# The order of part products in the last down unit of each MLP round

## The chip, the cores and the metric

The kernel runs on one core of a Trainium2 chip. The metric is device time in microseconds (us), as the median of several executions. TensorE does the matrix products (PE in the profile, its weight loads PEld), VectorE (DVE), ScalarE (ACT) and GpSimd (POOL) do the rest, and SyncE (SP) issues most transfers.

## What is computed

One inference step of a decoder with two layers, for 512 prompt tokens and 64 sample tokens that share all weights (576 columns, model width 1024). Each layer is a mixer and an MLP, each with a norm ahead and a residual behind:

```
hp = hp + yp                       # mixer 0: retention and gating, mixer 1: windowed attention
hp = hp + sqrelu_mlp(rmsnorm(hp, norm_mlp[l]), mlp_w_up[l], mlp_w_down[l])

def sqrelu_mlp(h, w_up, w_down):
    return jnp.square(jax.nn.relu(h @ w_up)) @ w_down     # width 1024 -> 4096 -> 1024
```

The change is in the product with `w_down`.

## The kernel before

Activations lie with features on the 128 partitions and the 576 tokens along the free axis, in two halves of 288 (`TH`). Every matrix product is made in float32r from two parts per operand: a value is `hi` (rounded by a cast on ScalarE) plus `lo` (the rest, a subtraction on VectorE), and hi·hi, hi·lo and lo·hi are added up in PSUM. `block` (L304) does this for a whole 576-column product, `product` (L311) for one of 288 columns.

Weights arrive as raw tiles (three buffers). Each piece of 128x512 is a job: ScalarE casts it to `whi` (L248), VectorE subtracts to get `wlo` (L259). `whi` and `wlo` have six buffers each (`NW_ = 6`), so the cast of job n+6 waits until TensorE has read job n to the end. `ahead_to(used + 5)` after each product prepares one job more; sums of weight blocks (L233, on VectorE) stand ahead of some casts.

Each MLP runs in four rounds of 1024 hidden features. A round has eight up products of 48 matmuls and then four down units `m = 0..3`. A down unit is a block product in the Strassen manner: seven products P1, P5, P6, P2, P7, P3, P4, each of 12 matmuls of 128x128 on 128x288: four blocks `k` of hidden features times three pairs of parts. `w` is the job's `whi` and `wlo`, `x(k)` the parts `ahi` and `alo` of block k's squared activations. Between products ScalarE copies accumulators (L548, L554, L561) and VectorE adds them into the residual `h` (L512). The first unit (`m = 0`) takes blocks 0 to 2 first and block 3 later. The last round of the second MLP has no down units, so there are seven rounds with a last unit (`m = 3`): four in the first MLP, three in the second. Rounds are counted here from 0 within the first MLP.

In the last round of the first MLP the norm of mixer 1 is prepared between the products: for each chunk c of `h`, ScalarE makes `xhi` (L391) and the square (L401), VectorE makes `xlo` (L392), and GpSimd adds the square into `ssq` (L407). Then mixer 1 starts with a `block` product over the eight chunks and with `norm.finish()`, which casts `ssq` to `sqh` (ScalarE, L212), subtracts `sql` (VectorE, L213) and multiplies both by a matrix of ones (L370, L371). `bq` (L958) is a small scaling of a bias on VectorE that belongs to mixer 1.

Inside the MLPs VectorE and ScalarE run in the order in which the code is written; TensorE, and everything in mixer 1, runs in the order of a scheduler.

Of the kernel before, what the change touches and what calls it, by code (L numbers as in the profile page):

```python
# [18 lines left out]
P = 128  # L19
D = 1024  # L20
KC = D // P
# [99 lines left out]
def hybrid_step(ctx: ExitStack, tc: tile.TileContext, a, o):  # L121
    nc = tc.nc
# [11 lines left out]
    def acc_tile():  # L134
        return ps.tile([P, 2, 512], F32, name="acc", tag="acc", bufs=2)

    def m_tile(name="m"):
        return ps.tile([P, 512], F32, name=name, tag="m", bufs=4)
# [12 lines left out]
    for c in range(KC):  # L151
        t = keep.tile([P, T], F32, name=f"h{c}")
# [119 lines left out]
    def ahead_to(n):  # L272

        n = min(n, len(jobs))
        while len(parts) < n or owed:
            while summed[0] < min(len(parts) + 2, len(jobs)):
                job, i = jobs[summed[0]]
                k = SUMS.get(job)
                if k:
                    total(k, i)  # L280
                summed[0] += 1
            if len(parts) < n:
                prepare()
            split_low()
        load_to(done[0] + 3)

    def take(n):
        i = used[0]
        used[0] += n
        split_to(i + n)  # L290
        return parts[i:i + n]
# [12 lines left out]
                nc.tensor.matmul(out, lhsT=w_, rhs=x_[:, hf if isinstance(hf, slice) else half(hf)],  # L304
                                 start=(start and si == 0), stop=(stop and si == 2))

    def product(out, w, x, ks_, start, stop):

        for si, (wi, xi) in enumerate(((0, 0), (0, 1), (1, 0))):
            for k in ks_:  # L310
                nc.tensor.matmul(out, lhsT=w[wi][:, k * P:(k + 1) * P], rhs=x(k)[xi],  # L311
                                 start=(start and k == ks_[0] and si == 0),
                                 stop=(stop and k == ks_[-1] and si == 2), skip_group_check=True)

    def cut(piece, k):
        return [w[:, (k % 4) * P:(k % 4 + 1) * P] for w in piece[k // 4]]
# [176 lines left out]
    def down_unit(acts, m, first, between, nxt):  # L493


        operand = {"P1": 0, "P2": 2, "P3": 1, "P5": 3, "P6": 4, "P7": 5, "P4": 6}
        row1, row2 = h[2 * m], h[2 * m + 1]
        both = acc_tile()
        x, v = both[:, 0, 0:TH], both[:, 1, 0:TH]
        n2, n1 = slice(0, TH), slice(TH, T)  # L500

        def bank(name):
            return m_tile(name)[:, 0:TH]

        def run(n, out, start, stop=True, ks_=range(4), w=None, ahead=NW_ - 1):
            w = w or take(1)[0]
            product(out, w, lambda k: [t[:, operand[n]] for t in acts[k]], ks_, start, stop)
            if ahead:
                ahead_to(used[0] + ahead)

        def to_h(row, cols_, src, op):
            nc.vector.tensor_tensor(out=row[:, cols_], in0=row[:, cols_], in1=src, op=op)  # L512

        def shared(src):
            to_h(row1, n2, src, ALU.add)
            to_h(row2, n2, src, ALU.subtract)

        if first:

            y, g, f = bank("y"), bank("g"), bank("f")  # L520
            early = [("P1", x), ("P2", y), ("P3", g), ("P5", f)]
            ws = take(4)
            for (n, out), w in zip(early, ws):
                run(n, out, True, False, range(3), w, 0)
            for (n, out), w in zip(early, ws):
                run(n, out, False, True, [3], w, 0)
                if n == "P1":
                    nc.scalar.copy(out=v, in_=x)
            to_h(row1, n1, y, ALU.add)
            to_h(row1, n2, g, ALU.add)  # L530
            ahead_to(used[0] + 2)
            run("P6", x, False, ahead=0)
            shared(f)
            z = bank("z")
            nc.scalar.copy(out=z, in_=x)
            ahead_to(used[0] + 2)
            to_h(row1, n1, v, ALU.add)
            to_h(row1, n2, x, ALU.add)
            w_ = bank("w")
            run("P4", w_, True, ahead=3)  # L540
            to_h(row2, n1, w_, ALU.subtract)
            run("P7", z, False, ahead=4)
            to_h(row2, n1, z, ALU.subtract)
            to_h(row2, n2, z, ALU.subtract)
            return
        run("P1", x, True)
        y = bank("y")
        nc.scalar.copy(out=y, in_=x)  # L548
        f = bank("f")
        run("P5", f, True)  # L550
        shared(f)
        run("P6", x, False)
        z = bank("z")
        nc.scalar.copy(out=z, in_=x)  # L554
        for c in between[0:1]:
            nxt.chunk(c)
        run("P2", y, False)
        to_h(row1, n1, y, ALU.add)
        run("P7", z, False)
        w_ = bank("w")  # L560
        nc.scalar.copy(out=w_, in_=z)  # L561
        to_h(row2, n2, z, ALU.subtract)
        for c in between[1:2]:
            nxt.chunk(c)
        run("P3", x, False)
        to_h(row1, n2, x, ALU.add)
        run("P4", w_, False)
        to_h(row2, n1, w_, ALU.subtract)
# [774 lines left out]
```

## Time and profile before

| | |
|---|---|
| median of 3 runs | 1242.55 us (1240.84 to 1244.82) |
| the profiled execution | 1244.38 us, span 1242.3 us |
| TensorE busy (matmul / weight load) | 97% / 96% |
| VectorE, ScalarE, GpSimd busy | 69%, 47%, 15% |
| mean granted TensorE clock | 0.993 of full speed |
| chain that ended last | TensorE 82%, VectorE 10%, ScalarE 3%, issue 3%, DMA 2% |
| matmuls in `product` (L311) | 2352, of which 588 in last units |

The timeline lists instructions by their start; the length of a matmul there includes its way through the array, so the pace is read from the distance of two starts. A number in brackets at the end of a row is idle time of that engine just before it, with what ended it.

### The profile page before, as it was taken

To read this page: it belongs to the slowest core of one execution; us is meant where nothing else is said; L and a number is where in the kernel's file an instruction comes from. 1 tells how busy PE (TensorE), PEld (TensorE's weight loads), DVE (VectorE), ACT (ScalarE), POOL (GpSimd) and SP (SyncE) were. 2 spreads that over 40 slices of the span, in tenths; PEclk is the share of its full clock that TensorE was granted. 3 is DMA by queue.
4 is the path that set the end of the run, shared out by engine and by line. 5 is a ranking of instruction groups with operands and counts; after the bars stand their busy time and mean duration, and the time that the engine had idled before them with its cause. 6 is when DMAs were issued, how large, how long until landed. Compare 5 with 4: busy or idle time off the path is not lost.

```text
span 1242.3 us, 22717 instructions
## 1 busy us (share of the span) xinstructions
PE 1205.8 (97%) x9213; PEld 1187.3 (96%) x9213; DVE 852.9 (69%) x1546; ACT 581.2 (47%) x1101; POOL 192.2 (15%) x166
## 2 busy tenths in 40 slices
PE   8999999999999999999999999999999999999996
PEld 8999999999999999999998999999999999999996
DVE  8867785456856866875886778546885784784455
ACT  5333454344434434444465777444443443443363
POOL 3543330110000000000013553220000000001223
PEclk9999999999999999999999999999999999999998
DMA  8244222222232242242133212122142233123253
GB/s 280 88 135 121 73 82 75 85 69 85 69 119 68 69 120 86 53 135 69 58 96 107 69 37 68 52 85 69 51 123 82 69 102 102 52 87 118 85 152 112
DMA packets 38521, 113.62 MB, mean 91 GB/s; under 512 B 4161, under 2 KB 11521, under 8 KB 38401
## 3 DMA queue, kind: packets, MB, share of 16 engines
q1 hardware_dynamic: 37408, 110.31, 29.2%
q8 instruction: 72, 1.18, 0.4%
q0 software_dynamic: 320, 1.31, 0.3%
q10 hardware_dynamic: 688, 0.55, 0.2%
q14 instruction: 33, 0.26, 0.1%
HBM read 107.12 MB, written 6.03 MB: 91 GB/s over the span
## 4 chain that ended last, share of the span: by engine, by line
PE 82%; DVE 10%; ACT 3%; issue 3%; DMA 2%; SPq 0%; DVEq 0%; POOL 0%; ACTq 0%
PE acc L304 54%; PE acc L311 7%; PE dn L304 4%; DVE wlo L259 3%; PE y L311 3%; PE w L311 2%; PE f L311 2%; PE z L311 2%; DMA raw<-in_w_dn 1%; DVE s L233 1%; DVE h L512 1%; DVE xlo L392 1%; PE g L311 1%; PE tpp L1089 1%; ACT whi L248 1%
## 5 line engine op out<-in xcount | busy, mean ns | idle before, releaser
L304 PE MATMUL acc<-xhi,whi 128*128 128x288 f32 x1520 | 329.2, 298 | 0.4 <-DVE vz L704 0.4
L304 PE MATMUL acc<-xlo,whi 128*128 128x288 f32 x1520 | 325.7, 296 | 2.4 <-DVE xlo L392 2.4
L304 PE MATMUL acc<-xhi,wlo 128*128 128x288 f32 x1520 | 326.1, 296 | 0.0
L259 DVE TENSOR_TENSOR wlo<-raw,whi 128x512 fp32r<-128x512 f32 x340 | 250.3, 749 | 90.0 <-ACT whi L248 88.1
L248 ACT CAST whi<-raw 128x512 fp32r<-128x512 f32 x340 | 202.9, 617 | 151.8 <-PE acc L304 115.0
L304 PEld LDWEIGHTS acc<-xlo,whi 128*128 128x128 f32 x1520 | 245.2, 189 | 2.7 <-DVE xlo L392 2.7
L304 PEld LDWEIGHTS acc<-xhi,whi 128*128 128x128 f32 x1520 | 244.6, 189 | 1.8 <-issue 1.4
L304 PEld LDWEIGHTS acc<-xhi,wlo 128*128 128x128 f32 x1520 | 245.4, 189 | 0.3
L462 ACT ACTIVATE q<-t 128x576 f32<-128x576 f32 x64 | 43.9, 686 | 241.8 <-DVE t L457 241.8
L407 POOL TENSOR_TENSOR ssq<-ssq,sq 128x576 f32<-128x576 f32 x25 | 37.2, 1489 | 511.7 <-ACT sq L401 511.5
L457 DVE SCALAR_TENSOR_TENSOR t<-acc,rstd 128x576 f32<-128x576 f32 x64 | 48.3, 755 | 94.6 <-PE acc L304 94.4
L248 ACT CAST whi<-s 128x512 fp32r<-128x512 f32 x112 | 66.0, 618 | 74.3 <-DVE s L233 61.3
L259 DVE TENSOR_TENSOR wlo<-s,whi 128x512 fp32r<-128x512 f32 x112 | 75.6, 685 | 13.5 <-ACT whi L248 13.5
L473 DVE TENSOR_TENSOR alo<-q,ahi 128x864 fp32r<-128x864 f32 (+1 forms) x56 | 67.5, 1205 | 7.2 <-ACT ahi L472 7.2
L472 ACT CAST ahi<-q 128x864 fp32r<-128x864 f32 (+1 forms) x56 | 58.2, 1039 | 11.9 <-DVE q L480 11.0
L311 PE MATMUL acc<-ahi,whi 128*128 128x288 f32 x308 | 55.5, 298 | 7.8 <-ACT y L548 7.8
L465 POOL TENSOR_TENSOR alo<-q,ahi 128x576 fp32r<-128x576 f32 x8 | 11.4, 1430 | 332.5 <-ACT ahi L464 332.5
L233 DVE TENSOR_TENSOR s<-raw 128x512 f32<-128x512 f32 x56 | 40.9, 730 | 32.0 <-DMA raw<-in_w_dn 32.0
L311 PEld LDWEIGHTS acc<-ahi,whi 128*128 128x128 f32 x308 | 45.4, 188 | 9.7 <-ACT y L548 9.4
L311 PE MATMUL acc<-ahi,wlo 128*128 128x288 f32 x308 | 54.6, 295 | 0.0
L311 PE MATMUL acc<-alo,whi 128*128 128x288 f32 x308 | 54.5, 295 | 0.0
L304 PE MATMUL acc<-ohi,wlo 128*128 128x288 f32 x208 | 46.4, 296 | 0.0
(323 smaller groups left out, 2151.2 us busy)
## 6 DMA issues: line engine op xcount, KB each, us to landing
raw<-in_w_dn SPq DMA_DIRECT2D x72, 512.0 KB
raw<-in_w_up SPq DMA_DIRECT2D x64, 512.0 KB
raw<-in_w_in SPq DMA_DIRECT2D x22, 512.0 KB
raw<-in_w_o SPq DMA_DIRECT2D x16, 512.0 KB
raw<-in_w_qkv SPq DMA_DIRECT2D x10, 512.0 KB
h<-in_xT SPq DMA_DIRECT2D x8, 288.0 KB
s<-in_s SPq DMA_DIRECT2D x4, 512.0 KB
out_ret_s<-s SPq DMA_DIRECT2D x4, 512.0 KB
```

What stands on the lines that cost most here:

```text
L233: nc.vector.tensor_tensor(out=sums[k, i], in0=x, in1=b[y], op=ALU.add)
L248: nc.scalar.copy(out=hi, in_=src)
L259: nc.vector.tensor_tensor(out=lo, in0=src, in1=hi.bitcast(F32), op=ALU.subtract)
L304: nc.tensor.matmul(out, lhsT=w_, rhs=x_[:, hf if isinstance(hf, slice) else half(hf)], start=(start and si == 0), stop=(stop and si == 2))
L311: nc.tensor.matmul(out, lhsT=w[wi][:, k * P:(k + 1) * P], rhs=x(k)[xi], start=(start and k == ks_[0] and si == 0), stop=(stop and k == ks_ ...
L392: nc.vector.scalar_tensor_tensor(out=lo, in0=h[c], scalar=g, in1=hi.bitcast(F32), op0=ALU.mult, op1=ALU.subtract)
L407: nc.gpsimd.tensor_tensor(out=self.ssq, in0=self.ssq, in1=sq, op=ALU.add)
L457: nc.vector.scalar_tensor_tensor(out=halves(t), in0=view, scalar=0.0, in1=norm.rv, op0=ALU.max, op1=ALU.mult)
L462: nc.scalar.activation(out=flat(q[:, seg]), in_=t, func=AF.Square)
L472: nc.scalar.copy(out=hi[:, s0 - 1:s1 - 1], in_=q[:, s0:s1])
L473: nc.vector.tensor_tensor(out=lo[:, s0 - 1:s1 - 1], in0=q[:, s0:s1], in1=hi.bitcast(F32)[:, s0 - 1:s1 - 1], op=ALU.subtract)
L512: nc.vector.tensor_tensor(out=row[:, cols_], in0=row[:, cols_], in1=src, op=op)
```

## The change

`product` gets a switch `by_block`. Without it the order is as before: for each pair of parts all blocks k. With it, each block's three pairs follow each other: `whi·ahi`, `wlo·ahi`, `whi·alo`. `down_unit` sets the switch for `m == KC // 2 - 1`, the last unit of a round.

```
--- before.py
+++ after.py
@@ -304,13 +304,17 @@
-    def product(out, w, x, ks_, start, stop):
-
-        for si, (wi, xi) in enumerate(((0, 0), (0, 1), (1, 0))):
-            for k in ks_:
-                nc.tensor.matmul(out, lhsT=w[wi][:, k * P:(k + 1) * P], rhs=x(k)[xi],
-                                 start=(start and k == ks_[0] and si == 0),
-                                 stop=(stop and k == ks_[-1] and si == 2), skip_group_check=True)
+    def product(out, w, x, ks_, start, stop, by_block=False):
+
+
+        pairs = ((0, 0), (0, 1), (1, 0))
+        if by_block:
+            steps = [(k, s) for k in ks_ for s in ((0, 0), (1, 0), (0, 1))]
+        else:
+            steps = [(k, s) for s in pairs for k in ks_]
+        for n, (k, (wi, xi)) in enumerate(steps):
+            nc.tensor.matmul(out, lhsT=w[wi][:, k * P:(k + 1) * P], rhs=x(k)[xi], start=(start and n == 0),
+                             stop=(stop and n == len(steps) - 1), skip_group_check=True)
@@ -504,7 +508,7 @@
-            product(out, w, lambda k: [t[:, operand[n]] for t in acts[k]], ks_, start, stop)
+            product(out, w, lambda k: [t[:, operand[n]] for t in acts[k]], ks_, start, stop, m == KC // 2 - 1)
```

TensorE, round 1, product P1 of the last unit (`acc`; each `ahi` and `alo` with a number of its own is a block k, `whi` and `wlo` are one job). Before:

```order
L311 MATMUL acc_5111<-ahi_4149,whi_5029 128x288
L311 MATMUL acc_5111<-ahi_4280,whi_5029 128x288
L311 MATMUL acc_5111<-ahi_4415,whi_5029 128x288
L311 MATMUL acc_5111<-ahi_4552,whi_5029 128x288
L311 MATMUL acc_5111<-alo_4150,whi_5029 128x288
L311 MATMUL acc_5111<-alo_4281,whi_5029 128x288
L311 MATMUL acc_5111<-alo_4416,whi_5029 128x288
L311 MATMUL acc_5111<-alo_4553,whi_5029 128x288
L311 MATMUL acc_5111<-ahi_4149,wlo_5030 128x288 [waits DVE_49]
L311 MATMUL acc_5111<-ahi_4280,wlo_5030 128x288
L311 MATMUL acc_5111<-ahi_4415,wlo_5030 128x288
L311 MATMUL acc_5111<-ahi_4552,wlo_5030 128x288
```

The same product in the changed kernel:

```order
L316 MATMUL acc_5111<-ahi_4149,whi_5029 128x288
L316 MATMUL acc_5111<-ahi_4149,wlo_5030 128x288 [waits DVE_49]
L316 MATMUL acc_5111<-alo_4150,whi_5029 128x288
L316 MATMUL acc_5111<-ahi_4280,whi_5029 128x288
L316 MATMUL acc_5111<-ahi_4280,wlo_5030 128x288
L316 MATMUL acc_5111<-alo_4281,whi_5029 128x288
L316 MATMUL acc_5111<-ahi_4415,whi_5029 128x288
L316 MATMUL acc_5111<-ahi_4415,wlo_5030 128x288
L316 MATMUL acc_5111<-alo_4416,whi_5029 128x288
L316 MATMUL acc_5111<-ahi_4552,whi_5029 128x288
L316 MATMUL acc_5111<-ahi_4552,wlo_5030 128x288
L316 MATMUL acc_5111<-alo_4553,whi_5029 128x288
```

The first reader of `wlo`, with its wait on VectorE, moved from the ninth place to the second; the last reader of `whi` moved from the eighth place to the twelfth, that of `wlo` from the twelfth to the eleventh. The same holds in all 49 products of the seven last units; TensorE's order elsewhere is unchanged.

VectorE at the border from the first MLP to mixer 1 (`h_88` and `h_92` are chunks 6 and 7 of the residual). Before:

```order
L512 TENSOR_TENSOR h_92<-h_92,w 128x288
L392 SCALAR_TENSOR_TENSOR xlo<-h_88,cols,xhi 128x576
L958 TENSOR_SCALAR bq_7499<-cols 128x8
L259 TENSOR_TENSOR wlo<-raw,whi 128x512
L392 SCALAR_TENSOR_TENSOR xlo<-h_92,cols,xhi 128x576
L259 TENSOR_TENSOR wlo<-raw,whi 128x512
L213 TENSOR_TENSOR sql<-ssq,sqh 128x576
```

In the changed kernel:

```order
L516 TENSOR_TENSOR h_92<-h_92,w 128x288
L962 TENSOR_SCALAR bq_7499<-cols 128x8
L259 TENSOR_TENSOR wlo<-raw,whi 128x512
L396 SCALAR_TENSOR_TENSOR xlo<-h_88,cols,xhi 128x576
L396 SCALAR_TENSOR_TENSOR xlo<-h_92,cols,xhi 128x576
L259 TENSOR_TENSOR wlo<-raw,whi 128x512
L213 TENSOR_TENSOR sql<-ssq,sqh 128x576
```

The `xlo` of chunk 6 moved behind `bq` and one `wlo`. It is the only change of order on VectorE; ScalarE, GpSimd and SyncE keep theirs.

## Rows read from the trace of the kernel before

**Rows 1.** Page, part 1: busy time, share of the span, instructions per engine.

```profile
PE 1205.8 (97%) x9213; PEld 1187.3 (96%) x9213; DVE 852.9 (69%) x1546; ACT 581.2 (47%) x1101; POOL 192.2 (15%) x166
```

**Rows 2.** TensorE's waits, longest first: total us, times, longest us.

```profile
PE acc L311 <- ACT y L548: 7.8, 7, 1.1
PE w L311 <- ACT w L561: 4.5, 8, 2.0
PE acc L304 <- DVE xlo L392: 2.7, 2, 2.4
```

**Rows 3.** TensorE in the windows of the seven last units: us in all, busy.

```profile
sum 78.12, PE 78.12; mean PE 11.16
```

**Rows 4.** Timeline, TensorE, last unit of round 1: start us, us, instruction, count.

```profile
444.12 0.69 PE L311 MATMUL acc<-ahi,whi 128*128 128x288 f32 x4
444.65 0.69 PE L311 MATMUL acc<-alo,whi 128*128 128x288 f32 x4
...
455.24 0.43 PE L304 MATMUL acc<-xhi,whi 128*128 128x288 f32 x2
```

**Rows 5.** Timeline, TensorE, first unit of round 1, block 3 alone.

```profile
413.61 0.29 PE L311 MATMUL acc<-ahi,whi 128*128 128x288 f32 x1
...
415.20 0.70 PE L311 MATMUL acc<-ahi,whi 128*128 128x288 f32 x4
```

**Rows 6.** Timeline, TensorE, mixer 1, where the granted clock is half.

```profile
665.09 0.68 PE L304 MATMUL acc<-xhi,whi 128*128 128x288 f32 x2
665.57 0.61 PE L304 MATMUL acc<-xlo,whi 128*128 128x288 f32 x2
```

**Rows 7.** Timeline, VectorE: wlo of P1 (round 1), of P6 and P2 (round 3).

```profile
440.75 0.69 DVE L259 TENSOR_TENSOR wlo<-raw,whi 128x512 fp32r<-128x512 f32 x1
...
643.33 0.68 DVE L259 TENSOR_TENSOR wlo<-s,whi 128x512 fp32r<-128x512 f32 x1
...
645.02 0.68 DVE L259 TENSOR_TENSOR wlo<-raw,whi 128x512 fp32r<-128x512 f32 x1
```

**Rows 8.** Timeline, TensorE, last unit of round 3: starts of P6 and P2.

```profile
645.01 0.80 PE L311 MATMUL acc<-ahi,whi 128*128 128x288 f32 x4
...
646.69 0.70 PE L311 MATMUL y<-ahi,whi 128*128 128x288 f32 x4
```

**Rows 9.** Timeline, ScalarE, end of the last unit of round 1 and after it.

```profile
454.90 0.62 ACT L248 CAST whi<-raw 128x512 fp32r<-128x512 f32 x1 [0.96 <-DVE wlo L259]
462.63 0.68 ACT L462 ACTIVATE q<-t 128x576 f32<-128x576 f32 x1 [7.11 <-DVE t L457]
```

**Rows 10.** Timeline, VectorE at the border to mixer 1, and a small scaling later.

```profile
656.81 0.80 DVE L392 SCALAR_TENSOR_TENSOR xlo<-h,cols,xhi 128x576 fp32r<-128x576 f32 x1
657.54 1.43 DVE L958 TENSOR_SCALAR bq<-cols 128x8 f32<-128x8 f32 x1
658.89 0.68 DVE L259 TENSOR_TENSOR wlo<-raw,whi 128x512 fp32r<-128x512 f32 x1
659.49 1.95 DVE L392 SCALAR_TENSOR_TENSOR xlo<-h,cols,xhi 128x576 fp32r<-128x576 f32 x1
...
831.20 0.16 DVE L592 TENSOR_SCALAR gfin<-cols 128x8 f32<-128x8 f32 x1
```

**Rows 11.** Timeline, GpSimd at the border: the last two adds of squares.

```profile
657.45 1.49 POOL L407 TENSOR_TENSOR ssq<-ssq,sq 128x576 f32<-128x576 f32 x1 [4.14 <-ACT sq L401]
659.02 1.80 POOL L407 TENSOR_TENSOR ssq<-ssq,sq 128x576 f32<-128x576 f32 x1
```

**Rows 12.** Timeline, TensorE at the border: chunk 6, chunk 7, `sql`.

```profile
658.11 0.43 PE L304 MATMUL acc<-xlo,whi 128*128 128x288 f32 x2
661.49 0.54 PE L304 MATMUL acc<-xlo,whi 128*128 128x288 f32 x2 [2.42 <-DVE xlo L392]
662.76 0.61 PE L371 MATMUL ms<-sql,ones_dr 128*128 128x288 f32 x1 [0.34 <-DVE sql L213]
```

**Rows 13.** Window: us long, TensorE busy, granted clock, DMA share, GB/s.

```profile
662.56:665.97 3.41, 3.21 (x13) 0.50 0.49 123
```

## The prediction

> **What bounds the kernel now.** I read the page's busy times first: TensorE's matmuls cover 97% of the span and no other engine passes 69% [rows 1]. So the time moves only if TensorE's work gets longer or shorter, or if its few waits do. Next its waits, longest first [rows 2]: inside the down units it waits for two ScalarE copies of accumulators, never for a `wlo`, although a wait on VectorE stands in front of the `wlo` matmuls. Then the seven last units, which the change rewrites: their windows add up to 78.12 us, all busy [rows 3]. Four matmuls take 0.53 us there (444.12 to 444.65) and the 84 of round 1 take 455.24 - 444.12 = 11.12 us, so 0.1324 us each [rows 4]. There is no idle time in these units to win, apart from a little before P6 in round 3. Last I read the place where the order of another engine changes: the border to mixer 1, where TensorE waits 2.42 us for an `xlo` and then 0.34 us for `sql` [rows 12].
>
> **The change, part by part.** Nothing is added or removed: the same 588 matmuls, weight loads, casts and copies. Four things move.
>
> *The pace.* In a last unit each matmul now differs from its neighbour in the weights (as before), and the second of each three reuses the right operand of the first. The nearest rows are those of block 3 in a first unit, where the three pairs of one block already follow each other: twelve single matmuls from 413.61 to 415.20, 1.59 us, 0.1325 each [rows 5]. That is the pace of rows 4 to 0.0001 us, so I take 0 for the sum. Their pairs come in the order hi·hi, hi·lo, lo·hi, so a repeated right operand is not in them; I bound that from below. At half clock two matmuls take 665.57 - 665.09 = 0.48 us [rows 6], 0.24 each; half of that, 0.12, is what one could take at full clock with no gap. If all 588 lost the gap, the gain would be 588 x 0.0124 = 7.3 us; if only the 196 that repeat an operand did, 2.4 us. Above, the bound is the second rival's price. I take 0 because rows 5 are the same instructions in nearly the same order.
>
> The Trainium skill ("TensorE: Matmul & The Clock Gate", section "Back-to-back issue gap") gives N/2.4 + 2.5 ns for an isolated stream, which for 288 columns would be an estimated 122.5 ns against the 132.4 ns of rows 4; by it the most the new order could win is an estimated 588 x 9.9 ns = 5.8 us. The trace shows 132 ns in either order, and nothing in it bears that gain out.
>
> *The wait for `wlo`.* It moves from the ninth matmul of a product to the second, so 7 x 0.132 = 0.93 us of cover go. What hides it is the distance that the jobs run ahead. In round 1 the `wlo` of P1 ends at 440.75 + 0.69 = 441.44, 2.68 us before P1 starts. The tightest are in round 3, where the norm's work lies between the products: P6's ends at 644.01, 1.00 us before its start at 645.01, and P2's at 645.70, 0.99 us before 646.69 [rows 7, 8]. These two are the smallest of the 49, counted off job by job in the timeline. With the one matmul ahead of the reader, the smallest margin is 0.99 + 0.13 = 1.12 us: cost 0. Were the cover gone, each us of lateness would cost TensorE a us.
>
> *The release of `whi`.* Its last reader moves from the eighth to the twelfth matmul, 4 x 0.132 = 0.53 us later. The cast that waits for it is ScalarE's job n+6. In round 1 the cast at 454.90 starts 0.2 us after P4's eighth matmul (P4 ends at 455.24 [rows 4, 9]), so now at about 455.44. Behind it in ScalarE's queue stands the square at 462.63, which is idle 7.11 us anyway because it waits on VectorE's `t`, and that on the next up product [rows 9]. Up to five casts of each unit shift so. A shifted cast starts 0.2 us after a product's end and takes 0.62 us; the copies `z` and `w` behind it wait for the end of the next product, 1.59 us after that, so 0.77 us are spare. Job n+6 itself is read only after five more products, 5 x 1.59 = 7.9 us after the release. VectorE's subtractions shift with the casts, by 0.5 us at most, ahead of waits for TensorE. SyncE's weight loads behind them move by as much and are not waited for there. In round 3 only the last cast is concerned, because the others already start after their product's end. Cost 0. `wlo` itself comes free one matmul earlier.
>
> *The border.* On VectorE `xlo` of chunk 6 goes behind `bq` and a `wlo`. Rows 10 and 11 must be read together. `bq` takes 1.43 us at 657.54, where a scaling of the same form takes 0.16 elsewhere: it started after GpSimd's add of 657.45 and ended as that add ended, at 658.94. `xlo` of chunk 7 started at 659.49, after the add of 659.02, and ended at 661.44, 0.62 us after that add's end (660.82). The `wlo` at 658.89 started before the add and was not held up; the add was, 1.80 instead of 1.49 us. So who starts first keeps the other waiting. Now the new order: `bq` at 656.81 runs freely, 0.16 us, and the next instruction starts 0.07 us before its end (as `bq` does behind `xlo`); `wlo` at 656.90, `xlo` of chunk 6 0.60 us later at 657.50, 0.05 us after the add of 657.45. It is held to 658.94 and ends at 659.56, where before the `wlo` ended at 659.57. So the second add ends at about 660.82 again, `xlo` of chunk 7 at 661.44 again, and `sql` follows as before. TensorE needs `xlo` of chunk 6 at 658.11 [rows 12] and gets it at 659.6: a new wait of 1.5 us, which is taken off the one of 2.42 us behind it. Cost 0.0. If instead `xlo` of chunk 6 starts first by a few hundredths, it ends at 658.2, the first add 1.25 us later at 659.4 (as 660.82 follows 659.57), `xlo` of chunk 7 at 660.1 and the second add at 661.3. From that add to the matmul with `sql` it was 662.76 - 660.82 = 1.94 us, so that matmul would come at 663.2 at the latest. So 0.0 to +0.5 us, and I take 0.0.
>
> The Trainium skill ("SBUF — State Buffer", section "🔬 SBUF: two separate sides") states this as an exclusive lock between GpSimd and a VectorE instruction with two SBUF inputs: whichever starts first holds it for the whole instruction. By that rule the 0.05 us between 657.45 and 657.50 decide between 0.0 and the +0.5 us, and the trace agrees with it, 1.43 against 0.16 us for the small scaling [rows 10, 11].
>
> **The sum**: 0 + 0 + 0 + 0.0 on the profiled execution, 1244.4 us with its span of 1242.3. That execution is 1.8 us above the median of the runs, so for the median I forecast 1242.6 us.
>
> **The rivals.**
>
> *Slower: the wait near a product's start.* After a wait TensorE's start is rough: P6 of round 3, behind a copy, shows 0.80 us for its first four matmuls instead of 0.69 [rows 4, 8]. If a wait on VectorE at the second matmul, even a satisfied one, keeps its weight load from running ahead, each of the 49 products loses about 0.1 us: 4.9 us, 1247.5 us. Against it: before, the same satisfied wait stands at the ninth matmul, and no gap shows there: the whole unit runs at 0.1324, as the single matmuls without it. It decides where the wait holds up the weight load, or where a `wlo` comes over 1.12 us later than now.
>
> *Faster: the repeated right operand hides the gap.* 196 matmuls win up to 0.0124 us each: 1240.2 us, which is within 0.3%; only if all 588 win would it be 1235.3. Against it: weight loads and matmuls are separate instructions in every row, and the pace of L311 doesn't depend on the order in rows 4 and 5.
>
> *The clock at the border.* From 662.56 to 665.97 the granted clock is 0.50, the lower of the two levels (1.2 of 2.4 GHz), right behind the waits of rows 12 [rows 13]. The one long wait now becomes two. If the dip goes, up to half of its 3.41 us comes back: 1.7 us, 1240.9; if another comes, as much is lost. The idle time in the stretch stays the same, so I expect the dip.
>
> *The change does nothing it says.* The order of instructions shows all 49 products rewritten, so this is left only as the case that the time is that of before.
>
> **How the numbers follow.** The forecast (all moves covered) 0.79; the wait that costs 0.06; the repeated operand 0.04, mostly small; the clock or the border by up to 1.7 us either way 0.11. 0.3% of 1242.55 is 3.7 us, about what a measurement of this kernel can tell from no change. Beyond it lie most of the first rival (slower 0.06) and a part of the second (faster 0.03); same 0.91. The range: downward the lowest run of before less the clock's 1.7 us, 1240.84 - 1.7 = 1239.1; upward half way from the highest run, 1244.82, to the slow rival's 1247.5, so 1246.1.
>
> **What would show it.** Right: the windows of the last units still add up to 78.1 us, without a wait on `wlo` L259 in TensorE's list; casts of `whi` at a unit's end start 0.5 us later and nothing behind them does; at the border two waits of about 1.5 and 1.0 us in place of 2.42, `bq` at 0.16 us, and `sql`'s matmul at the same distance from the unit's end. Wrong: units longer by 0.7 us each (the slow rival), a pace under 0.13, or a wait on `wlo` in round 3.

## The result, and the profile after

The changed kernel takes 1234.98 us (median of 5 runs, 1232.71 to 1237.24). Five runs of the kernel before had a median of 1243.80 (1240.84 to 1244.82). The ratio is 0.9939, with an interval of 0.9924 to 0.9955: faster by 0.6%, where no change was forecast, and below the range. Six more runs later gave a ratio of 0.9931 [0.9916, 0.9947].

The profiled execution took 1236.07 us with a span of 1234.0, 8.3 us less than the span of before. The page of the changed kernel, part 1 (busy time, share of the span, instructions):

```profile
PE 1199.2 (97%) x9213; PEld 1180.0 (96%) x9213; DVE 854.1 (69%) x1546; ACT 582.3 (47%) x1101; POOL 192.2 (16%) x166
```

Against [rows 1] TensorE is busy 6.6 us less with the same 9213 matmuls, so most of the gain is not waiting time. TensorE's waits, longest first (total us, times, longest us):

```profile
PE acc L316 <- ACT y L552: 7.5, 7, 1.1
PE w L316 <- ACT w L565: 3.7, 8, 2.0
...
PE acc L304 <- DVE xlo L396: 1.8, 4, 0.8
```

They stand nearly as in [rows 2], and no `wlo` is among them. The windows of the seven last units, the only place where TensorE's order changed, come next: two of them and their sum (columns as in [rows 13], matmul count in brackets).

```profile
346.17:357.34 11.17, 11.17 (x86) 1.00 0.54 149
...
638.81:650.28 11.47, 11.47 (x85) 0.97 0.43 116
...
sum 78.49, PE 78.49; mean PE 11.21
```

The sum is 78.49 us against 78.12 [rows 3]: the rewritten units are not faster. The time is gone from the stretches right behind six of them, the eight up products of the next round, 384 matmuls, whose order is the same in both kernels. (The last unit of round 3 is followed by mixer 1.) The windows of these six stretches, the first and the sum; before:

```profile
357.61:408.81 51.20, 51.20 (x386) 1.00 0.26 82
...
sum 307.20, PE 307.20; mean PE 51.20
```

After:

```profile
357.34:407.26 49.92, 49.92 (x387) 1.00 0.26 84
...
sum 299.51, PE 299.51; mean PE 49.92
```

The granted clock is 1.00 and TensorE is busy all the time in both, yet a matmul takes 51.20 / 384 = 0.1333 us before and 49.92 / 384 = 0.1300 after. That is 307.20 - 299.51 = 7.69 of the 8.3 us. The timeline shows how (each row is two matmuls, a pair; up products of round 1). Before:

```profile
403.48 0.43 PE L304 MATMUL acc<-xlo,whi 128*128 128x288 f32 x2
403.75 0.42 PE L304 MATMUL acc<-xhi,wlo 128*128 128x288 f32 x2
404.01 0.43 PE L304 MATMUL acc<-xhi,whi 128*128 128x288 f32 x2
404.29 0.42 PE L304 MATMUL acc<-xlo,whi 128*128 128x288 f32 x2
404.55 0.43 PE L304 MATMUL acc<-xhi,wlo 128*128 128x288 f32 x2
```

After:

```profile
401.80 0.42 PE L304 MATMUL acc<-xhi,whi 128*128 128x288 f32 x2
402.06 0.42 PE L304 MATMUL acc<-xlo,whi 128*128 128x288 f32 x2
402.32 0.42 PE L304 MATMUL acc<-xhi,wlo 128*128 128x288 f32 x2
```

After, every pair starts 0.26 us behind the last. Before, the distances are 0.27, 0.26, 0.28, 0.26: every other pair comes 0.01 to 0.02 us late, and so through 384 matmuls. The row ahead of a late pair is 0.43 us long, that ahead of the others 0.42. I call the two the long rhythm (0.1333) and the short rhythm (0.1300); the expectations quoted below call them slow and fast.

### The profile page after: what moved, and what is told of

It is laid out like the page before. It is cut to its first block, busy times and chain, and to the rows that moved or that the text cites. A ratio compares the mean times of both kernels' runs of the same rounds, so it can differ in the third digit from the quotient of the medians.

```text
span 1234.0 us, 22717 instructions
## 1 busy us (share of the span) xinstructions
PE 1199.2 (97%) x9213; PEld 1180.0 (96%) x9213; DVE 854.1 (69%) x1546; ACT 582.3 (47%) x1101; POOL 192.2 (16%) x166
## 4 chain that ended last, share of the span: by engine, by line
PE 81%; DVE 9%; ACT 3%; DMA 3%; issue 3%; SPq 0%; DVEq 0%; POOL 0%; ACTq 0%
PE acc L304 54%; PE acc L316 7%; PE dn L304 4%; DVE wlo L259 3%; PE w L316 3%; PE f L316 3%; PE y L316 2%; DMA raw<-in_w_dn 2%; PE z L316 2%; DVE h L516 1%; DVE s L233 1%; PE tpp L1093 1%; PE op L1106 1%; PE g L316 1%; ACT whi L248 1%
## 5 line engine op out<-in xcount | busy, mean ns | idle before, releaser
L304 PE MATMUL acc<-xhi,whi 128*128 128x288 f32 x1520 | 325.8, 296 | 0.3 <-DVE vz L708 0.3
L304 PEld LDWEIGHTS acc<-xhi,whi 128*128 128x128 f32 x1520 | 242.1, 188 | 1.8 <-issue 1.3
L316 PE MATMUL acc<-ahi,whi 128*128 128x288 f32 x308 | 65.6, 298 | 7.5 <-ACT y L552 7.5
L316 PE MATMUL acc<-ahi,wlo 128*128 128x288 f32 x308 | 65.0, 296 | 0.0
L316 PE MATMUL acc<-alo,whi 128*128 128x288 f32 x308 | 64.8, 295 | 0.0
L316 PEld LDWEIGHTS acc<-ahi,whi 128*128 128x128 f32 x308 | 49.0, 189 | 9.3 <-ACT y L552 9.2
L316 PEld LDWEIGHTS acc<-ahi,wlo 128*128 128x128 f32 x308 | 49.1, 189 | 0.0
```

## The experiments

"The six stretches" are those of the windows above.

**Which part of a last unit matters.** Two kernels split the change: only the last product of the unit, P4, by block, and all products but P4.

```
-            product(out, w, lambda k: [t[:, operand[n]] for t in acts[k]], ks_, start, stop, m == KC // 2 - 1)
+            product(out, w, lambda k: [t[:, operand[n]] for t in acts[k]], ks_, start, stop, m == KC // 2 - 1 and n == "P4")
```

> Only P4, the last product of a last unit, goes block by block; P1 to P3 and P5 to P7 keep the old order. In the trace after the change the up products that follow such a unit take 6.24 us per 48 matmuls instead of 6.40. Theory of the entry: TensorE's up stage keeps one of two rhythms, chosen by how TensorE comes out of the last product. Then six rounds of up products (48 products) run at 130.0 ns a matmul, 48 x 0.16 = 7.7 us are won, and the time is about 0.994 of before. Rival, the casts and waits: the later release of whi and the earlier wait for wlo in all seven products shift the other engines, and that frees TensorE. Then one seventh of the effect is left, about 1.1 us, and the up products stay near 133.3 ns. Rival, the whole unit has to run in the new order: up products at 133.3 ns, time as before.

Measured 0.9955 [0.9935, 0.9974], a median of 1235.9 us. Two of its six stretches, the first and the fifth (the last is the sum of all six):

```profile
358.37:408.29 49.92, 49.92 (x387) 1.00 0.28 84
...
1020.63:1071.81 51.18, 51.18 (x386) 1.00 0.27 82
...
sum 300.76, PE 300.76; mean PE 50.13
```

Five of six are in the short rhythm. So twelve matmuls per round carry most of the gain, but with the same twelve ahead one stretch still took the long rhythm.

```
+            product(out, w, lambda k: [t[:, operand[n]] for t in acts[k]], ks_, start, stop, m == KC // 2 - 1 and n != "P4")
```

> The six products P1, P5, P6, P2, P7, P3 of a last unit go block by block, P4 keeps the old order. Theory of the entry: up products stay at 133.3 ns a matmul (6.40 us per 48), time 1.000 of before. Rival, the casts and waits: six sevenths of the gain, about 6.6 us, time 0.995 of before.

Measured 1.0013 [0.9998, 1.0028], and all six stretches in the long rhythm:

```profile
sum 307.20, PE 307.20; mean PE 51.20
```

Six of seven products by block gain nothing. With them fall the causes that all seven products would share: earlier waits, later releases, a repeated operand.

**Order of the pairs, or by block.** The change does two things at once: it goes by block, and it swaps the second and third pair. One kernel goes by block with the old pairs, one goes pair by pair with the new ones.

```
-            steps = [(k, s) for k in ks_ for s in ((0, 0), (1, 0), (0, 1))]
+            steps = [(k, s) for k in ks_ for s in pairs]
```

> All seven products of a last unit go block by block, but within a block the pairs keep the old order: whi with ahi, whi with alo, wlo with ahi. No two neighbours share the right operand any more; the last matmul of a unit reads wlo. Theory of the entry: it depends on where TensorE comes out, which can't be told beforehand; if interleaving the blocks suffices, 130.0 ns a matmul and 0.994 of before. Rival, the repeated right operand (whi with ahi, then wlo with ahi) is what does it: 133.3 ns and 1.000 of before.

Measured 0.9939 [0.9916, 0.9963], the full gain:

```profile
sum 299.49, PE 299.49; mean PE 49.91
```

Here `xlo` of chunk 6 stands ahead of `bq` as before, and `bq` takes 1.43 us as in [rows 10] (start 653.69), so the new order on VectorE is not needed for the gain either.

```
+            steps = [(k, s) for s in ((0, 0), (1, 0), (0, 1)) for k in ks_]
```

> All seven products of a last unit go pair by pair as before, but with the pairs in the new order: all blocks for whi with ahi, then for wlo with ahi, then for whi with alo. Only the last four matmuls, and which weights they read, differ from before in kind. If the weights of the last matmul (whi, not wlo) choose the rhythm of the up products, they run at 130.0 ns and the time is 0.994 of before; if the interleaving of blocks does, they stay at 133.3 ns and the time is 1.000 of before.

Measured 1.0001 [0.9986, 1.0016], and the long rhythm in all six:

```profile
sum 307.20, PE 307.20; mean PE 51.20
```

Going by block in the last product is what counts, whichever pair comes second, and whichever part of the weights is the last in the array.

**The gain without the change.** If the up products only carry on with a rhythm that something started, something else should start it too. This is the kernel before, with one odd block per round: in the first block of the third up product the three matmuls of one half come first, then the three of the other, instead of the halves in turn.

```
+        steps = [(si, i) for si in range(3) for i in range(len(outs))]
+        if by_half:
+            steps.sort(key=lambda s: s[1])
...
-                    view = up()
+                    view = up(p == 1 and j == 0)
```

> The kernel before, with one block of six matmuls changed in each of the eight rounds: the first block of the third up product makes all three pairs of one token half before the other half (instead of the halves in turn). Down units are as before. Theory, two rhythms of TensorE that keep themselves up until something odd comes by: the first two up products of a round still take 6.40 us per 48 matmuls, and behind the odd block the rhythm is drawn anew: 6.24 us in some or all rounds (6 products, 0.96 us each round, up to 6 to 7 us in all). Rival, only the order of the down products can do it (something that they leave behind): 6.40 us before and behind, time as before.

One execution: 1235.76 us, against 1242.85 for the kernel before beside it. The first three up products of round 1, 48 matmuls each:

```profile
357.39:363.79 6.40, 6.40 (x51) 1.00 0.47 153
363.79:370.19 6.40, 6.40 (x51) 1.00 0.29 76
370.19:376.44 6.25, 6.25 (x50) 1.00 0.02 9
```

6.40 / 48 is 0.1333; the third product, which begins with the odd block, takes 6.25, and those behind it 6.24, 0.1300 each. The same happened in seven of eight rounds, round 2 staying in the long rhythm. So the short rhythm appears with the down units of before, from six matmuls in another order. The six stretches are 307.20 - 302.44 = 4.76 us shorter; where the rest of the 7.1 us between the two times comes from, one execution does not tell.

The next kernel puts every up block in half order, to see whether that order has a pace of its own.

> The kernel before, with all blocks of all up products in that half order: three matmuls in a row into one bank, then three into the other. Theory of two rhythms: the up products take another rhythm of their own, between the 130.0 and 133.3 ns a matmul that the halves in turn show and the 132.4 to 133 ns of the down products, which stay in one bank; if they stay in one bank's rhythm, 6.37 us per 48 in every round and -1.5 us in all. Rival, a rhythm is left behind by the down units whatever the ups are: 6.40 us in the rounds behind a down unit, as before.

Measured 1.0008 [0.9994, 1.0021], with the pace of the long rhythm in all six:

```profile
sum 307.14, PE 307.14; mean PE 51.19
```

The mean is that of the long rhythm, but in the timeline the matmuls follow each other evenly, 0.13 to 0.14 us apart, without late pairs. So half order is not itself the quicker order: what the kernel with one odd block won, it won behind that block, in blocks of the old order. The next kernel puts a single extra matmul (the ones matrix on half a chunk, overwritten at once) ahead of the third up product, which shifts everything behind it by one place.

```
+            if nudge:
+                nc.tensor.matmul(acc[:, 0, 0:TH], lhsT=ones_dr, rhs=norm.xs[0][0][:, half(0)], start=True, stop=True)
```

> The kernel before, with one matmul more in each of the eight rounds: a product of the matrix of ones with half a chunk, ahead of the third up product, into the bank that this product then overwrites. Theory of two rhythms: one odd matmul can turn the slow rhythm into the fast one, so behind it 6.24 us per 48 in some or all rounds, and the extra 8 x 0.13 us are paid back several times. Rival, the rhythm hangs on the order of the weights and halves and an extra matmul changes nothing: 6.40 us per 48, time 1.1 us above before.

One execution: 1245.86 us, with 51.31 or 51.32 us for each of the six stretches, of which the extra matmul is 0.13. In round 0, which had entered the short rhythm by itself, it did the opposite of help (second and third up product; all later ones take 6.40):

```profile
267.23:273.47 6.24, 6.24 (x50) 1.00 0.01 3
273.47:279.87 6.40, 6.40 (x51) 1.00 0.25 82
```

So not every disturbance helps, and the short rhythm can be lost. In the seven rounds that came in the long rhythm the extra matmul left it as it was.

**Again, and with help.** The changed kernel was run again, beside one with three odd blocks more: in the third up product of round 0 of the second MLP, and in one product of each mixer's output projection.

> The changed kernel as it is, once more, beside the next kernel on one chip. Theory of two rhythms: up products at 6.24 us per 48 matmuls in the six rounds behind a last unit, as in its first profile, and 0.994 of before. If the rhythm were drawn by chance in each execution, single rounds would be at 6.40.

0.9931 [0.9916, 0.9947], 1234.03 us; the six stretches again add up to 299.51. Round 0 of the first MLP, behind mixer 0 and not behind a last unit, was in the long rhythm this time; in the first profile of the same kernel it was in the short one from the second product on. So that entry differs from execution to execution of one kernel.

```
-                    view = up()
+                    view = up(r == 0 and p == 1 and j == 0 and nxt is None)
...
-                add_residual(dc, gemm(outs))
+                add_residual(dc, gemm(outs, nudge=dc == 0))
...
-                    view = gemm(outs)
+                    view = gemm(outs, nudge=dc == 2)
```

> The changed kernel with three odd blocks more (six matmuls in half order, as in the run with the half order once): in the first product of mixer 0's output projection, in the third product of mixer 1's, and in the third up product of the second MLP's first round. These stretches ran at 133.3, 132.9 and 133.3 ns a matmul. Theory of two rhythms: behind each odd block 130.0 ns: 8 products of mixer 0 and 6 up products at 0.16 us each, 2.2 us, and 6 products of mixer 1 at 0.13, 0.8 us; 3 us below the changed kernel, 0.992 of before. Where the odd block meets a stretch that other work holds up, nothing; and the first up products of the first MLP, fast before, may fall to 6.40 because their entry changes (1.1 us back). Rival, only down units leave a rhythm behind: as the changed kernel.

0.9919 [0.9904, 0.9935], 1232.98 us (1231.43 to 1235.01), the best of all, though its interval overlaps that of the changed kernel. The odd block in the up products worked (round 0 of the second MLP, products 2 and 3; the rest take 6.24):

```profile
833.46:839.86 6.40, 6.40 (x50) 1.00 0.00 0
839.86:846.12 6.26, 6.26 (x51) 1.00 0.27 88
```

Six products at 0.14 to 0.16 us less are 0.94 us. The odd blocks in the output projections changed nothing there (0.133 us per matmul). Two odd blocks in each of these projections were the next try.

> As the kernel with three odd blocks, but with two odd blocks in each output projection, in other places: blocks 3 and 6 of the first and third product of mixer 0's, blocks 3 and 6 of the fourth and sixth product of mixer 1's. If the place within the rhythm decides whether an odd block turns it, one of them gets through and a part of these projections falls from 133.3 and 132.9 to 130.0 ns a matmul, up to 1.6 us in all. If something in the projections holds the slow rhythm (the residual's add or the norm's work beside them), they stay, and the time is that of the kernel with three odd blocks.

One execution, 1235.98 us. Behind the second odd block mixer 0's projection ran at 0.130 us per matmul, that of mixer 1 stayed at 0.133. Round 0 of the first MLP, which follows, began in the short rhythm this time and then fell out of it (first and second up product; the rest take 6.40):

```profile
259.86:266.11 6.25, 6.25 (x51) 1.00 0.29 84
266.11:272.50 6.39, 6.39 (x50) 1.00 0.01 3
```

The five products won in the projection gave 0.8 us, and round 0 took 310.90 - 259.34 = 51.56 us against 310.83 - 260.22 = 50.61 in the profile with three odd blocks, so nothing was left. Since the entry there differs between executions anyway, one execution doesn't tell whether the odd blocks caused the loss. Most of the 3 us between these two profiles arose later, in mixer 1: round 1 begins at 357.46 and 357.31, the second MLP at 829.71 and 826.53. The changed kernel's own two profiles differ there as well (829.27 and 827.06), so that part says nothing of the odd blocks.

**Does an odd block lead to the short rhythm, or turn the rhythm over?** The changed kernel with an odd block in the third up product of all eight rounds.

> The changed kernel with the odd block (six matmuls in half order) ahead of the third up product in all eight rounds. In six of them TensorE comes to it in the fast rhythm, in the first round of each MLP in the slow one. If the odd block always leads into the fast rhythm: 6.24 us per 48 matmuls behind it in all rounds. If it only draws the rhythm anew or turns it over: some or all of the six fast rounds fall to 6.40 behind it, and the time rises by up to 6 x 0.96 us above the changed kernel.

One execution, 1242.34 us, and 305.16 us in the six stretches: 5.65 of the 7.69 us are gone. Round 1, products 2 and 3, and round 0 of the second MLP, products 2 and 3:

```profile
364.45:370.69 6.24, 6.24 (x51) 1.00 0.20 72
370.69:377.07 6.38, 6.38 (x50) 1.00 0.04 15
...
840.41:846.82 6.41, 6.41 (x51) 1.00 0.00 0
846.82:853.07 6.25, 6.25 (x51) 1.00 0.27 88
```

In all seven rounds that were in the short rhythm the odd block turned it into the long one (6.40 from the fourth product on), and in the one that was in the long rhythm it turned that into the short one. Of the two outcomes expected, that it always leads to the short one fell: it can turn the rhythm over either way.

**Where the odd block stands in the long rhythm.** The traces show what parts the odd blocks that ended the long rhythm from those that did not. In the kernel before with one odd block per round, these are the last row ahead of the odd block and its first matmul, in round 1, which turned, and in round 2, which did not:

```profile
369.92 0.43 PE L308 MATMUL acc<-xhi,wlo 128*128 128x288 f32 x2
370.19 0.29 PE L308 MATMUL acc<-xhi,whi 128*128 128x288 f32 x1
...
466.69 0.42 PE L308 MATMUL acc<-xhi,wlo 128*128 128x288 f32 x2
466.95 0.29 PE L308 MATMUL acc<-xhi,whi 128*128 128x288 f32 x1
```

In the seven rounds that turned the odd block stands where a late pair would have begun (0.43 in the row ahead); in round 2 the late pair had come just before it (0.42). The same sign parts the other six odd blocks that met this rhythm: 0.43 ahead of the four that turned it (one in round 0 of the second MLP in each of the last three kernels, and the second in mixer 0's projection), 0.42 ahead of the two in mixer 0's projection that changed nothing. That is 11 against 3 without an exception (mixer 1's projection, 6.38 us per 48 matmuls, runs in another pattern and is not counted). The one stretch that P4 alone did not bring into the short rhythm fits as well: P4 begins there two matmuls further behind the last late start than ahead of the other five. All 36 stretches behind units that go by block from the first product on, in six profiles, begin in the short rhythm. This is read from the traces; no run moved an odd block by one pair on purpose.

| kernel | six stretches, us | ratio, or time of one execution |
|---|---|---|
| before | 307.20 | 1 |
| changed | 299.51 | 0.9939 |
| only P4 by block | 300.76 | 0.9955 |
| all but P4 by block | 307.20 | 1.0013 |
| by block, old pairs | 299.49 | 0.9939 |
| pair by pair, new pairs | 307.20 | 1.0001 |
| before, one odd block | 302.44 | 1235.76 us |
| before, all up blocks odd | 307.14 | 1.0008 |
| before, extra matmul (six more matmuls counted) | 307.89 | 1245.86 us |
| changed, again | 299.51 | 0.9931 |
| changed, three odd blocks | 299.51 | 0.9919 |
| changed, more odd blocks | 299.52 | 1235.98 us |
| changed, odd block in every round | 305.16 | 1242.34 us |

## Why the prediction was wrong, and where it was right

**The step that failed is "The pace".** It asked what the new order does to the 588 matmuls that are rewritten, and there its 0 was nearly right: 78.49 against 78.12 us, of which 0.17 us lie in round 3's unit, at a clock of 0.97. It took the pace of all other matmuls as given, since their order stays, and gave no other reason. But the 6 x 384 = 2304 matmuls behind the last units were the ones with something to win: 6 x 1.28 = 7.7 us. The rows for it were in reach. In the kernel before, round 0 of the first MLP already ran its up products at 0.1300 us from the second one on (windows of its first two; the rest take 6.24):

```profile
261.08:267.48 6.40, 6.40 (x50) 1.00 0.29 82
267.48:273.72 6.24, 6.24 (x51) 1.00 0.01 3
```

Those of round 1, with the same instructions and the same clock, took 6.40 each. I compared the paces of products with each other, and not the pace of one kind of product from round to round. None of the signs that were to show the forecast wrong looked at the up products either.

By the Trainium skill ("TensorE: Matmul & The Clock Gate", section "Back-to-back issue gap") isolated matmuls of 288 columns would take an estimated 122.5 ns each; the same section sets that formula apart from a stream of weight loads and matmuls, which this is, and does not offer it as a bound for one. The best pace that any run here shows for these matmuls over a stage is 130.0 ns, and the last units themselves stay at 133 ns in either order; the 5.8 us that the estimate offered there did not come, and the 7.7 us came elsewhere.

**The repeated operand**: its size, up to 7.3 us, is by chance that of the gain, but it is not the cause. The kernel with the old pairs has no repeated right operand and the full gain.

**The wait for `wlo` and the release of `whi`: right.** No wait on `wlo` shows, and six of seven products by block cost nothing that can be measured (1.0013). ScalarE at the end of round 1's last unit (after):

```profile
453.80 0.62 ACT L248 CAST whi<-raw 128x512 fp32r<-128x512 f32 x1 [0.97 <-PE w L316]
460.83 0.69 ACT L466 ACTIVATE q<-t 128x576 f32<-128x576 f32 x1 [6.41 <-DVE t L461]
```

The cast now waits for `w` of L316 and starts 0.20 us after the unit's end (453.60), where it stood 0.34 us ahead of the end in [rows 4, 9]: 0.54 us later, as worked out. The square behind it is still idle 6.41 us.

**The slow rival** (the wait near a product's start) did not come: 0.1 us for each of 49 products would have made the windows 83 us.

**The border: the mechanism right, the waits smaller.** VectorE, GpSimd and TensorE at the border (after):

```profile
652.98 0.16 DVE L962 TENSOR_SCALAR bq<-cols 128x8 f32<-128x8 f32 x1
653.05 0.68 DVE L259 TENSOR_TENSOR wlo<-raw,whi 128x512 fp32r<-128x512 f32 x1
653.66 3.91 DVE L396 SCALAR_TENSOR_TENSOR xlo<-h,cols,xhi 128x576 fp32r<-128x576 f32 x2
...
653.62 3.32 POOL L411 TENSOR_TENSOR ssq<-ssq,sq 128x576 f32<-128x576 f32 x2 [3.11 <-ACT sq L405]
...
655.72 0.53 PE L304 MATMUL acc<-xlo,whi 128*128 128x288 f32 x2 [0.34 <-DVE xlo L396]
...
657.62 0.54 PE L304 MATMUL acc<-xlo,whi 128*128 128x288 f32 x2 [0.84 <-DVE xlo L396]
...
658.89 0.40 PE L375 MATMUL ms<-sql,ones_dr 128*128 128x288 f32 x1 [0.34 <-DVE sql L213]
```

`bq` takes 0.16 us, as forecast, and `xlo` of chunk 6 starts 0.04 us after GpSimd's add (forecast 0.05) and is held up behind it: the two `xlo` take 3.91 us together. This is what the Trainium skill ("SBUF — State Buffer", section "🔬 SBUF: two separate sides") says of a VectorE instruction with two SBUF inputs, and the trace agrees with it: `xlo` has two (`bq`, which the prediction named here, has one). The two new waits are 0.34 and 0.84 us instead of 1.5 and 1.0, and the matmul with `sql` stands 658.89 - 650.28 = 8.61 us behind the unit's end; before it was 662.76 - 653.05 = 9.71 us [rows 12], with the unit's end at the end of its window, 653.05.

VectorE did not come sooner: from the start of round 3's down units to the instruction behind VectorE's last add into `h` it is 652.98 - 599.87 = 53.11 us, before 656.81 - 604.11 = 52.70. TensorE came later to the unit's end, after 650.28 - 599.87 = 50.41 us instead of 653.05 - 604.11 = 48.94, because it ran at a granted clock of 0.53 for a while ahead of the unit (next paragraph). Two other runs have the old order on VectorE; these are their waits for the last `xlo`, by block with the old pairs, and the kernel before with one odd block per round:

```profile
657.64 0.53 PE L304 MATMUL acc<-xlo,whi 128*128 128x288 f32 x2 [2.53 <-DVE xlo L396]
...
659.74 0.54 PE L308 MATMUL acc<-xlo,whi 128*128 128x288 f32 x2 [1.35 <-DVE xlo L396]
```

The first has no dip ahead of the unit's end, and `sql`'s matmul 658.91 - 649.23 = 9.68 us behind it; the second has the dip there and 661.01 - 652.37 = 8.64 us. So the forecast was right that the new order on VectorE costs nothing, and the 1.1 us less came with the dip's new place.

**The clock**: the dip at the border is gone, and another one stands ahead of the last unit of round 3, behind the wait of 2.04 us before the third unit's last product, a wait that was there before with the clock at 1.00 behind it. The stretch behind that wait before, and, after, the same stretch and the one behind `sql`'s matmul:

```profile
640.06:643.47 3.41, 3.41 (x25) 1.00 0.16 66
...
635.89:639.30 3.41, 3.41 (x15) 0.53 0.14 54
658.89:662.30 3.41, 3.41 (x25) 1.00 0.48 132
```

With 15 matmuls instead of 25 behind the wait, and 25 instead of 13 [rows 13] behind `sql`'s matmul, about as much was lost at the one place as was won at the other. From the start of these down units to the second MLP it is 829.27 - 599.87 = 229.40 us, before 833.14 - 604.11 = 229.03, so in these two profiles border and clock together hold nothing of the gain. I had expected the dip to stay where it was; the kernel by block with the old pairs has it at the border, and the kernel before with one odd block per round has it ahead of the last unit, so its place does not follow the order of the last unit.

## What to carry to other kernels

When the order of matmuls is changed, read the pace of the unchanged matmuls behind them as well, over whole stages, and compare stages of the same code with each other: two paces at the same granted clock and without idle time may be a gain to be had. Here the way in decides between them, so a few matmuls in another order were worth 7.7 us, and one more odd block per round took 5.65 of them back; such a gain has to be read again from the trace after every edit ahead of it.

## What the runs showed that was not expected

TensorE ran one and the same stream of weight loads and matmuls (128x128 on 128x288, granted clock 1.00, no idle time) at 0.1333 or at 0.1300 us per matmul, 2.5% apart, and mostly kept to it for whole stages of 50 us. Shown are: a last unit all by block was followed by the short rhythm (36 of 36 stretches in six profiles), with P4 alone by block by the short one in 5 of 6, and with P4 by pair by the long one (18 of 18 in three profiles: the kernel before, all but P4, and pair by pair with the new pairs); one odd block turned the short rhythm into the long one in 7 of 7 rounds, and the long one into the short one at 11 of 14 places, namely those where a late pair would have begun; behind mixer 0 either rhythm came, from execution to execution. What in the chip holds the rhythm, why the order of the last twelve matmuls and the place of an odd block choose it, and why an extra matmul ended the short one once and the long one never, stays open; no run was made on these.
